# Hybrid decoder step on Trainium2: output-gate projections moved to the end and done in pairs by seven block products

## The chip, the cores and the metric

One core of a Trainium2 chip runs the whole program. The metric is the device time of one execution in microseconds, the median of several runs. The engines of the core work side by side, each through its own queue in order: TensorE (PE) multiplies matrices, VectorE (DVE) and ScalarE (ACT) do elementwise work, GpSimd (POOL) more of it, and SyncE (SP) issues the DMA transfers.

## The reference

One layer is applied to a prompt group (512 tokens) and a sample group (64 tokens); the kernel treats them as 576 tokens side by side.

```
proj = x @ w_in                       # 2048 -> 21904 columns
y_a = rwkv7(proj[..., :o1])           # RWKV-7 time mixing, 16 heads of 64
y_b = sliding_window_attention(...)   # y_c = mlstm(...), y_d = retention(...)
z    = silu(proj[..., o4:o5])         # 4 branches x 1024
gate = sigmoid(proj[..., o5:])        # 4 branches x 2048
for i, y_i in enumerate((y_a, y_b, y_c, y_d)):
    merged += gate[:, :, i] * ((y_i * z[:, :, i]) @ w_branch[i])
x_new = layer_norm(ALPHA * x + merged @ w_out)
```

In RWKV the state follows S <- S * w + sa (kk a)^T + v k^T token by token, with sa = -S kk. The kernel does this in chunks of 64 tokens, for which it needs the inverse of I + M1, M1 a strictly triangular 64 by 64 matrix for each head and chunk.

## The kernel before

**The projections.** w_in is cut into tiles of 128 columns; 171 of them are projections of x, among them 32 for z and 64 for the gates. x is kept on the chip transposed, as a high and a low part in float32r (xh, xl, 16 blocks of 128 rows). A projection (`dense_steps`, line 1285) loads its weights in two halves of 512 KB (raw, line 1297), splits each quarter in a high part on ScalarE (wh, line 1280) and a low part on VectorE (wl, line 1281), and multiplies: for each of 16 row blocks wh xh, wh xl and wl xh, each on two halves of the tokens of 288 columns, 96 matmuls in all, into one PSUM tile psd of two banks. One of the 16 row blocks, six matmuls, is a **step**.

**The stream.** Projections are one stream that TensorE works on between the mixers' own small products. `pump(n)` (line 1373) takes n steps. When a projection ends the next is taken from `asked`, the list that the mixers fill with projections of their own, or, if that is empty, from `work`: the 32 z and then the 64 gates, which wait for nothing. Each step of pump also advances `side`, a generator of other work, and what is left of finished projections. `need(name)` (line 1404) pumps until a projection is done. TensorE keeps the program's order, so a matmul that waits holds all that stand behind it, and pump is how other work is put in front of such a wait. The results of z and gates go to DRAM (zs, lines 1440 to 1456) and come back in phase 2. All DMAs here are issued by SP, in order: an issue that waits for its data holds the weight loads behind it.

**The RWKV mixer** (`branch_a`, line 198) takes two heads at a time, eight pairs j. `ask(j)` puts keys, receptances and values of the pair into `asked`. `prepare(j)` (line 282) makes normalised keys, decays and the array BK, with 32 steps of pump between its parts (FILL_SQUARES, FILL_SCAN, FILL_DECAY, FILL_NORM, FILL_BONUS) and needs for its own projections; the norms are taken to a power by GpSimd (nr). `grams(j)` (line 395) multiplies tokens against tokens, masks, sends M1 to DRAM (m1d) and reads it back to 126 partitions (MU, 3072 numbers each), 11 steps of pump in all. It then appends `invert` (line 367) to `side`: forward substitution on GpSimd, 63 rows, two instructions a row (lines tmp and TU), a row or so for each step of pump, then a store to DRAM (td, line 385) and loads into TT (line 390). `recur(j)` (line 486) first pumps until `side` is empty and then goes through eight chunks, each a chain of products with TT and the state and five steps of pump, and the sample group; 59 steps in all. Between prepare(j + 1) and recur(j) stand FILL_RECUR = 34 steps, and FILL_LAST = 110 ahead of the last recur.

**The other mixers** are sliding-window attention (line 589), mLSTM (841) and retention (1022). mLSTM and retention need a head's own projections at the head's start and ask for the next head's right behind that.

**The end.** What is left of `work` after retention runs while the first branch's inputs are loaded (`load_branch`, line 1484). Phase 2 multiplies the branches by w_branch (psd, line 1223), phase 3 is the output projection (pso) and the norm.

Of the kernel before, what the change touches and what calls it, by code (L numbers as in the profile page):

```python
# [19 lines left out]
P = 128  # L20
# [15 lines left out]
FIRST = {0: ("a_lo", 0), 1: ("a_k0", 0), 4: ("a_lo", 8)}  # L36
DECAY_C = 0.5 * float(np.exp(-0.5))

# [50 lines left out]
def _constants():  # L89
    """Tables that depend on shapes alone."""  # L90
# [18 lines left out]
    g, jj = i // 18, np.arange(10)  # L109
    c["tinit"] = (np.arange(64)[None, None] == (g[:, None] + 7 * jj[None])[:, :, None]).astype(f).reshape(P, 640)  # L110
# [37 lines left out]

CONST = _constants()
# [4 lines left out]
NG = 7  # L154
NJ = 10
# steps of the projections put between the steps of this branch
FILL_RECUR = 34
FILL_FIRST = 24
FILL_LAST = 110
# [38 lines left out]
def branch_a(S):  # L198
    with S.tc.tile_pool(name="bra", bufs=1) as pool:
        a = RwkvBranch(S, pool)  # L200
        a.prepare(0)
        S.pump(FILL_FIRST)
        a.grams(0)
        for j in range(8):
            if j < 7:
                a.ask(j + 1)
                a.prepare(j + 1)
                S.pump(FILL_RECUR)
            else:
                S.pump(FILL_LAST)  # L210
            a.recur(j)
            if j < 7:
                a.grams(j + 1)
        S.nc.sync.dma_start(out=S.O["o_shift"], in_=S.oshift)


class RwkvBranch:
    """Two heads at a time, in chunks of 64 tokens; the ninth chunk is the sample group.

    Rows of the arrays of a head pair: the even head's channels (or tokens) lie on partitions  # L220
    0..63 and the odd head's on 64..127; `ri` names the half that is not the head's own."""
# [6 lines left out]
    def __init__(self, S, pool):  # L228
# [7 lines left out]
        t = lambda name, shape: pool.tile([P] + shape, FP32, name=name)  # noqa: E731  # L236
# [3 lines left out]
        self.TT = t("TTbd", [9, 2, 64])  # L240
# [5 lines left out]
        for x in (self.TT, self.S0, self.U, self.Vb, self.Yn, self.bbd, self.kbd):  # L246
            S.G.memset(x, 0.0)
# [7 lines left out]
        self.ask(0)  # L255
# [8 lines left out]
    def ask(self, j):  # L264
        """the projections of a pair: keys, receptances and values (with 64 zeros on both sides)"""
        S = self.S

        def finish(n, col):
            def f(ps):
# [5 lines left out]
                x = self.tile("x" + n)  # L275
# [3 lines left out]
        for n, col in (("k", 8 + j), ("r", j), ("v", 16 + j)):  # L279
            S.ask(f"a_{n}{j}", finish(n, col), 256)  # L280

    def prepare(self, j):
# [4 lines left out]
        # normalised keys  # L287
# [14 lines left out]
        # decay and learning rate  # L302
# [10 lines left out]
        # running sums of the decays' logarithms  # L313
# [24 lines left out]
        r, vx = S.need(f"a_r{j}"), S.need(f"a_v{j}")  # L338
        v = vx[:, 64:64 + T]
# [5 lines left out]
        # bonus of the current token  # L345
# [4 lines left out]
        S.pump(FILL_BONUS)  # L350
        for a in range(0, T, SPL):
# [15 lines left out]
    def invert(self, st, mua, mub, tu, tmp):  # L367
        """forward substitution, one row of the unknowns' right side after another"""
        S, n = self.S, 18 * NG
        for _ in range(ROWS_BEFORE):  # L370
            yield 1
        for i in range(63):
            a = min(i // NG + 1, NJ)
            w = 63 - i
            row = mua[0:n, i, i + 1:64] if i < 32 else mub[0:n, i - 32, i - 31:32]
            S.tt(tmp[0:n, 0:a, 0:w], tu[0:n, 0:a, i:i + 1].to_broadcast([n, a, w]),
                 row.unsqueeze(1).to_broadcast([n, a, w]), eng=S.G)
            S.tt(tu[0:n, 0:a, i + 1:64], tu[0:n, 0:a, i + 1:64], tmp[0:n, 0:a, 0:w], ALU.subtract, eng=S.G)
            if i % ROWS_PACE == ROWS_PACE - 1:
                yield 1  # L380
# [3 lines left out]
        td = S.dpool.tile([18, NJ, NG, 64], FP32, tag="td", name="td", bufs=2)  # L384
# [3 lines left out]
        TT = self.TT  # L388
        for h in range(2):
            S.paced(S.nc.sync.dma_start(out=TT[self.HALF[h], :, h],  # L390
                                        in_=td[9 * h:9 * h + 9].rearrange("c a g t -> (a g) c t")[0:64]))
        for _ in range(ROWS_AFTER):
            yield 1

    def grams(self, j):
# [9 lines left out]
        m1 = self.tile("e3", (9, 64))  # L405
# [3 lines left out]
        for c0, n in ((0, 4), (4, 4), (8, 1)):  # L409
# [7 lines left out]
            for h in range(2):  # L417
# [4 lines left out]
                b1 = lambda x: x.unsqueeze(1).to_broadcast([64, n, 64])  # noqa: E731  # L422
                tt(m1[rs, c0:c0 + n], pv[rs, :, 0], b1(mk[rs, 0]))
# [7 lines left out]
        # inverse of I + M1, transposed: rows (group, head, chunk), each group every seventh row  # L431
        m1d = S.dpool.tile([18, 3072], FP32, tag="m1d", name="m1d", bufs=2)
        for h in range(2):
            d = m1d[9 * h:9 * h + 9]
            nc.sync.dma_start(out=d[:, 0:2048].rearrange("c (i t) -> i c t", i=32), in_=m1[64 * h:64 * h + 32])
            nc.sync.dma_start(out=d[:, 2048:].rearrange("c (i t) -> i c t", i=32),
                              in_=m1[64 * h + 32:64 * h + 64, :, 32:64])
        mu = self.tile("MU", (3072,))
        mua, mub = mu[:, 0:2048].rearrange("p (i t) -> p i t", i=32), mu[:, 2048:].rearrange("p (i t) -> p i t", i=32)
        tu = self.tile("TU", (NJ, 64))  # L440
        tmp = self.tile("tmp", (NJ, 64))
        nc.sync.dma_start(out=tu, in_=S.I["c_tinit"].rearrange("p (a b) -> p a b", a=NJ))
        nc.sync.dma_start(out=mu[0:18 * NG], in_=m1d.unsqueeze(0).broadcast_to([NG, 18, 3072]))
        S.side.append(self.invert(st, mua, mub, tu, tmp))
        # tokens on partitions
# [30 lines left out]
        # the sample group's queries, masked to each batch  # L476
# [9 lines left out]
    def recur(self, j):  # L486
        S, nc, st = self.S, self.S.nc, self.st.pop(j)
        V, G, act, tt, stt, mm, tr, pm = S.V, S.G, S.act, S.tt, S.stt, S.mm, S.tr, S.pm
        Z, BN, SV, TT, U, S0, dl = self.Z, self.BN, self.SV, self.TT, self.U, self.S0, st["dl"]
        while S.side:  # L490
            S.pump(1)
# [7 lines left out]
        two = lambda x: x.rearrange("p a b -> p (a b)")  # noqa: E731  # L499
# [29 lines left out]
        # the sample group  # L529
# [32 lines left out]
        # norm of each head (the even head's tokens on partitions 64..127)  # L562
# [26 lines left out]
def branch_b(S):  # L589
    nc, V, mm, tr, act, tt, stt, pm = S.nc, S.V, S.mm, S.tr, S.act, S.tt, S.stt, S.pm  # L590
    with S.tc.tile_pool(name="brb", bufs=1) as pool:
# [84 lines left out]
        def outputs(j, s):  # L676
            # probabilities with keys on partitions
# [29 lines left out]
        # the sample group: (KV head, query head, token) on partitions  # L707
# [46 lines left out]
def gate_rows(S, pool, dpool):  # L754
    """mLSTM gates, heads on partitions 0..7; returns the per-token rows the heads need"""
# [59 lines left out]
    # rows to every partition, by way of DRAM  # L815
# [4 lines left out]
    # tokens on partitions: [., 0:8] li - F, [., 32:40] weights of the state, [., 64:72] exp(-m)  # L820
# [20 lines left out]
def branch_c_heads(S, fmd, scd, cols):  # L841
    nc, V, mm, act, tt, stt, pm = S.nc, S.V, S.mm, S.act, S.tt, S.stt, S.pm
    with S.tc.tile_pool(name="brc", bufs=1, reuse_waits="tile") as pool:
# [4 lines left out]
        def conv(j, ps):  # L848
            """causal convolution of four taps and silu; twice its value"""
# [38 lines left out]
        for j in range(4):  # L888
            q2, k2 = S.need(f"c_q{j}"), S.need(f"c_k{j}")
            vcs = [S.need(f"c_v{2 * j + e}") for e in range(2)]  # L890
            if j < 3:
                ask(j + 1)
            # row factors on every partition
# [20 lines left out]
            # keys with tokens on partitions, weighted for the state  # L914
# [58 lines left out]
                # the sample group  # L973
# [27 lines left out]
def rope(S, pool, ps, cos, sin, half, name, bufs=2):  # L1001
    """x cos + (x with its halves swapped) sin, channels on partitions"""
# [19 lines left out]
def branch_d(S):  # L1022
    nc, V, mm, act, tt, stt, pm = S.nc, S.V, S.mm, S.act, S.tt, S.stt, S.pm
    with S.tc.tile_pool(name="brd", bufs=1) as pool:
# [18 lines left out]
        for h in range(8):  # L1043
            qr, kr, vc = S.need(f"d_q{h}"), S.need(f"d_k{h}"), S.need(f"d_v{h}")
            if h < 7:
                ask(h + 1)
            S.pump(6)
            # queries with their decay
# [5 lines left out]
            # keys and values with tokens on partitions  # L1054
# [14 lines left out]
            # scores, keys on partitions  # L1069
# [12 lines left out]
            # outputs, chunk after chunk, and the states  # L1082
# [19 lines left out]
            # the sample group: one state for each batch  # L1102
# [23 lines left out]
def head_out(S, pool, o, i, h, which, den=None):  # L1126
    """norm over the head's 128 values (tokens on partitions), transposed, gain and bias"""
# [33 lines left out]

@with_exitstack
def hybrid_kernel(ctx: ExitStack, tc: tile.TileContext, I, O):
# [3 lines left out]
    class InOrder:  # L1167
        """an engine whose instructions keep the order of the program"""
# [14 lines left out]
    class Behind:  # L1183
        """an engine whose instructions stay behind the last weight split before them"""
# [42 lines left out]
    def mm(out, lhsT, rhs, start=True, stop=True):  # L1227
# [495 lines left out]
```

## Time and profile before

| | us |
|---|---|
| median of 3 runs | 3391.16 |
| lowest to highest | 3389.91 to 3391.79 |
| span of the profiled execution | 3394.3 |

The profile is of one execution of its own; its span from the first to the last instruction is that execution's time, 3.1 us above the median of the runs. Stages as the trace has them, in us from the span's start: x comes in until about 32, RWKV until 1525, attention until 1814, mLSTM until 2231, retention until 2733, the rest of the stream until 2762, phase 2 until 3171, phase 3 to the end.

How to read the rows. In the table of windows a row has the stretch, its length, then for PE, PEld (weight load), DVE, ACT and POOL the busy us and the count of instructions, then the granted TensorE clock, the DMA engines' busy share and GB/s; with a filter on one tile and engine it has that engine alone. In the list of waits a row has who waited for whom, the total in us, how often and the longest. A group of instructions has line, engine, operation, output <- inputs, partitions x elements, count | busy us, mean ns of one | idle time before them and what ended it. In a timeline a row has start and duration in us and, in brackets, the idle time ahead of it. In the chain of work a row has start, length, engine and tile, and how many instructions were merged.

### The profile page before, as it was taken

What the parts mean: (1) busy time and instruction counts of PE and PEld (TensorE: products, weight loads), DVE (VectorE), ACT (ScalarE), POOL (GpSimd) and SP (SyncE); (2) the same over time, 40 slices, a digit from 0 to 9 for tenths busy, and PEclk for the clock granted to TensorE, in tenths of its full rate; (3) what the DMA queues carried; (4) which work ended last, traced back from release to release, by engine and by line L of the source; (5) the groups of instructions that cost most, each with busy time, mean ns of one, the idle gap of its engine ahead of it and who ended that gap; (6) DMA issues with size and microseconds to landing.
All of it is one profiled execution on the core that took longest, in us unless ns stands there. A gap on an engine that the chain in (4) does not pass through costs nothing.

```text
span 3394.3 us, 59113 instructions
## 1 busy us (share of the span) xinstructions
PE 3292.9 (97%) x24166; PEld 3160.5 (93%) x24166; DVE 1561.2 (46%) x3322; ACT 993.5 (29%) x2023; POOL 696.9 (21%) x1133
## 2 busy tenths in 40 slices
PE   8989998999899999999999999999999999999998
PEld 8979998989899899999999999999999999999886
DVE  5534454544444443334653455533343344555435
ACT  4323232323232323223443222222222222222211
POOL 0434435261708071611310000000000000000000
PEclk9989999999999999999999999999999999999999
DMA  5323232323231323334323333233333365554523
GB/s 166 110 82 108 95 115 84 113 89 111 87 106 63 115 91 107 112 101 133 93 90 107 94 96 95 88 123 119 101 102 115 97 197 184 184 171 132 171 79 106
DMA packets 174144, 384.67 MB, mean 113 GB/s; under 512 B 63704, under 2 KB 67544, under 8 KB 172272
## 3 DMA queue, kind: packets, MB, share of 16 engines
q1 hardware_dynamic: 173872, 380.88, 35.5%
q8 instruction: 190, 3.11, 0.4%
q14 instruction: 82, 0.67, 0.1%
HBM read 316.32 MB, written 58.11 MB: 110 GB/s over the span
## 4 chain that ended last, share of the span: by engine, by line
PE 73%; POOL 15%; DMA 6%; issue 3%; DVE 2%; SPq 1%; ACT 0%; POOLq 0%; ACTq 0%; DVEq 0%
PE psd L1177 45%; PE psd L1223 12%; PE pm L1177 10%; POOL TU L1177 7%; POOL tmp L1177 7%; PE pso L1223 6%; DMA MU<-m1d 3%; DMA raw<-in_wi 1%; DMA td<-TU 0%; POOL nr L1177 0%; DMA TTbd<-td 0%; DMA m1d<-e 0%; DMA raw<-in_wo 0%; DVE e L1193 0%; DVE wl L1281 0%
## 5 line engine op out<-in xcount | busy, mean ns | idle before, releaser
L1177 PE MATMUL psd<-xh,wh 128*128 128x288 f32 (+1 forms) x5472 | 1231.2, 306 | 10.1 <-ACT wh L1280 9.7
L1177 PE MATMUL psd<-xh,wl 128*128 128x288 f32 (+1 forms) x5472 | 1182.4, 297 | 31.7 <-DVE wl L1281 31.7
L1177 PE MATMUL psd<-xl,wh 128*128 128x288 f32 (+1 forms) x5472 | 1181.9, 297 | 0.0
L1281 DVE TENSOR_TENSOR wl<-raw,wh 128x512 fp32r<-128x512 f32 x812 | 595.7, 736 | 945.0 <-ACT wh L1280 928.9
L1280 ACT ACTIVATE wh<-raw 128x512 fp32r<-128x512 f32 x812 | 510.9, 631 | 1601.9 <-PE psd L1177 1218.0
L1177 PEld LDWEIGHTS psd<-xh,wl 128*128 128x128 f32 x5472 | 893.3, 190 | 33.7 <-DVE wl L1281 33.7
L1177 PEld LDWEIGHTS psd<-xh,wh 128*128 128x128 f32 x5472 | 883.4, 190 | 41.3 <-issue 14.5
L1177 PEld LDWEIGHTS psd<-xl,wh 128*128 128x128 f32 x5472 | 892.2, 190 | 0.0
L1177 POOL TENSOR_TENSOR tmp<-TU,MU 126x112 f32<-126x112 f32 (+49 forms) x504 | 262.7, 521 | 381.2 <-DMA MU<-m1d 342.9
L1177 POOL TENSOR_TENSOR TU<-TU,tmp 126x112 f32<-126x112 f32 (+49 forms) x504 | 263.5, 523 | 39.5
L1223 PE MATMUL psd<-yl,wh 128*128 128x288 f32 x1024 | 219.5, 295 | 0.0
L1223 PE MATMUL psd<-yh,wl 128*128 128x288 f32 x1024 | 219.4, 295 | 0.0
L1223 PE MATMUL psd<-yh,wh 128*128 128x288 f32 x1024 | 219.3, 295 | 0.0
L1177 POOL TENSOR_TENSOR rstd<-rstd,mhalf 128x5 f32<-128x5 f32 (+1 forms) x24 | 36.0, 1502 | 727.0 <-DVE rstd L1193 727.0
L1223 PEld LDWEIGHTS psd<-yh,wl 128*128 128x128 f32 x1024 | 164.6, 189 | 0.0
L1223 PEld LDWEIGHTS psd<-yh,wh 128*128 128x128 f32 x1024 | 164.6, 189 | 0.0
L1223 PEld LDWEIGHTS psd<-yl,wh 128*128 128x128 f32 x1024 | 164.6, 189 | 0.0
L1177 POOL TENSOR_TENSOR rs<-rs,mhalf 128x1 f32<-128x1 f32 (+1 forms) x5 | 4.5, 901 | 656.5 <-DVE rs L1193 656.5
L1177 POOL TENSOR_TENSOR smp<-Vbd,c_mrow 64x512 f32<-64x512 f32 x16 | 16.6, 1040 | 429.2 <-PE pm L1177 428.6
L1223 PE MATMUL pso<-w3h,mh 128*128 128x512 f32 x260 | 102.6, 395 | 1.4 <-ACT w3h L1193 1.4
L1223 PE MATMUL pso<-w3l,mh 128*128 128x512 f32 x260 | 103.3, 397 | 0.2 <-DVE w3l L1193 0.2
L1177 POOL TENSOR_TENSOR rsw<-rsw,c_sin 128x576 f32<-128x576 f32 x25 | 38.7, 1548 | 306.3 <-DMA rsw<-rx 306.3
(331 smaller groups left out, 2916.6 us busy)
## 6 DMA issues: line engine op xcount, KB each, us to landing
raw<-in_wi SPq DMA_DIRECT2D x342, 512.0 KB
raw<-in_wb SPq DMA_DIRECT2D x64, 512.0 KB
gd<-zs SPq DMA_DIRECT2D x64, 288.0 KB
th<-gd SPq DMA_DIRECT2D x64, 288.0 KB
raw<-in_wo SPq DMA_DIRECT2D x32, 512.0 KB
MU<-m1d SPq DMA_DIRECT2D x8, 1512.0 KB
zsd<-zs SPq DMA_DIRECT2D x32, 288.0 KB
ya<-yd SPq DMA_DIRECT2D x32, 288.0 KB
```

Of the source, the lines that this page charges most:

```text
L1177: ins = f(*a, **k).ins
L1223: PE.matmul(out=out, lhsT=lhsT, rhs=rhs, start=start, stop=stop)
L1280: a = nc.scalar.activation(out=wh, in_=src, func=ACTF.Copy)
L1281: b = nc.vector.tensor_tensor(out=wl, in0=src, in1=wh.bitcast(FP32), op=ALU.subtract)
```

## The change

RWKV: the FILL_RECUR and FILL_LAST steps go. Keys and receptances of pair j + 2 are asked for before recur(j), values of j + 1 at the start of grams(j). The part of the grams that gives M1 is computed a second time in a new `triangle`, right behind prepare, and the inversion starts from there, a recur and a grams ahead of its use (two TT buffers). The inversion is of two blocks of 32 (31 rows on 108 partitions, MU of 1024 numbers, 11 by 32 unknowns); the off-diagonal block is joined by nine transposes and two times 18 small products on TensorE. mLSTM and retention ask for the next head's projections before they need their own.

```diff
         a.prepare(0)
+        a.triangle(0)
+
+        a.ask(1, "kr")
         S.pump(FILL_FIRST)
         a.grams(0)
         for j in range(8):
             if j < 7:
-                a.ask(j + 1)
                 a.prepare(j + 1)
-                S.pump(FILL_RECUR)
-            else:
-                S.pump(FILL_LAST)
+
+                a.triangle(j + 1)
+            if j < 6:
+                a.ask(j + 2, "kr")
             a.recur(j)
...
-ROWS_BEFORE = 8
-ROWS_PACE = 5
-ROWS_STORE = 4
-ROWS_LOAD = 4
-ROWS_AFTER = 3
+ROWS_BEFORE = 18
+ROWS_STORE = 2
+ROWS_LOAD = 8
+ROWS_AFTER = 6
+ROWS_JOIN = 2
...
+        for c0, m in ((0, 4), (4, 4), (8, 1)):
+            ps = pm()
+            for c in range(m):
+                tr(ps[:, c * P:c * P + P], TT[:, c0 + c].rearrange("p a b -> p (a b)"), S.ident)
...
+                mm(ps[h][down[h], HB * c:HB * c + HB], m12[up[h], c], t11[up[h], c])
...
+                mm(ps[h][up[h], HB * c:HB * c + HB], g[down[h], c], TT[down[h], c, h, HB:64])
...
+    def triangle(self, j):
+
+        S, nc, st = self.S, self.S.nc, self.st[j]
+        V, act, tt, mm, pm = S.V, S.act, S.tt, S.mm, S.pm
+        while S.side:
+            S.pump(1)
+        m1 = self.tile("e3", (9, 64))
+        for c0, n in ((0, 8), (8, 1)):
+            S.pump(1)
+            ps = [pm() for _ in range(2)]
+            for c in range(n):
+                t0 = 64 * (c0 + c)
+                for h in range(2):
+                    rs = self.HALF[h]
+                    mm(ps[h][rs, 64 * c:64 * c + 64], st["bk"][rs, c0 + c, h], st["kk"][rs, t0:t0 + 64])
...
+        S.side.append(self.invert(self.TT[j % 2], mu, tu, tmp, m12))
...
-        while S.side:
+        while j == 7 and S.side:
             S.pump(1)
```

The stream's end: after retention two more projections run the old way (BEFORE_SEVEN = 2) while `input_forms` loads x again and makes four sums of its blocks, three of them as high and low parts at once. The rest of `work` goes to `Seven`. With two projections as rows of blocks A and the halves of x (rows and tokens) as blocks B, a pair is seven products of 8 row blocks, 288 tokens and three terms, fourteen units of 12 matmuls; four sums of weight blocks, 128 by 1024 numbers each in two instructions, are made by GpSimd, and results are summed by VectorE from two PSUM tiles and one more bank. Splits are made two units ahead. AFTER_SEVEN = 2, and one more where the number is odd, run singly while `load_branch(0)` loads.

```diff
+        b11, b12, b21, b22 = (x[:, i, j * SPL:j * SPL + SPL] for i in range(2) for j in range(2))
+        tm = pool.tile([P, 3, SPL], FP32, tag="tm", name="tm")
+        th, tl = (keep.tile([P, 3, SPL], F32R, name=f"{n}{k}") for n in ("fh", "fl"))
+        tt(t1[:, k], b12, b11, ALU.subtract, eng=G)
+        tt(tm[:, 1], b22, b12, ALU.subtract, eng=G)
+        tt(tm[:, 0], b22, t1[:, k], ALU.subtract)
+        tt(tm[:, 2], b21, tm[:, 0], ALU.subtract)
...
+        adds(u - 4, "S1", "A21", "A22", ALU.add, new=True)
+        adds(u - 2, "S2", "S1", "A11", ALU.subtract, new=True)
+        adds(u + 2, "A21", "A11", "A21", ALU.subtract)
+        adds(u + 4, "A12", "A12", "S2", ALU.subtract)
+
+        for src, b, which, first, last in (("A11", "B11", "X", 1, 0), ("A12", "B21", "Z", 1, 1),
+                                           ("S2", "T2", "X", 0, 0), ("S1", "T1", "W", 1, 0),
+                                           ("A21", "T3", "X", 0, 0), ("A12", "B22", "W", 0, 1),
+                                           ("A22", "T4", "X", 0, 1)):
...
+    rest = work[BEFORE_SEVEN:]
+    work[:] = work[:BEFORE_SEVEN]
+    with tc.tile_pool(name="conv", bufs=2, reuse_waits="tile") as vpool:
+        side.append(input_forms(S, vpool, tpool, seven, t1))
+        while side or work or len(current) > 1 or current[0][3] < 12:
+            pump(1)
+    spool = forms.enter_context(tc.tile_pool(name="blocks", bufs=1, reuse_waits="tile"))
+    stream = Seven(S, seven, t1, spool, evpool, rest)
+    stream.begin()
+    while current or finishing:
+        pump(1)
+    stream.pairs()
+    forms.close()
...
     ys = load_branch(0)
-    while current or work or finishing:
-        pump(1)
+    stream.tail()
```

More of the change, by code (lines that the diff above doesn't have):

```diff
@@ L146, in _constants @@
     return c
+HB = 32
+NG = 3
+NJ = 11
 CONST = _constants()
@@ L239, in __init__ @@
         self.SV = t("SV", [9, 2, 64])
-        self.TT = t("TTbd", [9, 2, 64])
+        self.TT = [t(f"TTbd{n}", [9, 2, 64]) for n in range(2)]
         self.S0 = t("S0bd", [8, P])
@@ L245, in __init__ @@
         self.bbd, self.kbd = t("bbd", [P]), t("kbd", [P])
-        for x in (self.TT, self.S0, self.U, self.Vb, self.Yn, self.bbd, self.kbd):
+        for x in (*self.TT, self.S0, self.U, self.Vb, self.Yn, self.bbd, self.kbd):
             S.G.memset(x, 0.0)
@@ L262, in tile, with ask @@
         return self.pool.tile([P] + list(shape), dt, tag=tag, name=tag, bufs=bufs)
-    def ask(self, j):
+    def ask(self, j, which):
         S = self.S
@@ L274, in f @@
                     return shift_mix(S, self.pool, ps, col, x[:, 64:64 + T], x)
-                x = self.tile("x" + n)
+                x = self.tile("x" + n, bufs=2 if n == "r" else 1)
                 return shift_mix(S, self.pool, ps, col, x, x)
             return f
-        for n, col in (("k", 8 + j), ("r", j), ("v", 16 + j)):
-            S.ask(f"a_{n}{j}", finish(n, col), 256)
+        for n in which:
+            S.ask(f"a_{n}{j}", finish(n, dict(k=8, r=0, v=16)[n] + j), 256)
     def prepare(self, j):
@@ L337, in prepare @@
             tt(kk[:, ts], kk[:, ts], ps[:, 0:ts.stop - ts.start])
-        r, vx = S.need(f"a_r{j}"), S.need(f"a_v{j}")
-        v = vx[:, 64:64 + T]
+        r = S.need(f"a_r{j}")
         t2 = sq
@@ L350, in prepare @@
         S.pump(FILL_BONUS)
+        vx = S.need(f"a_v{j}")
+        v = vx[:, 64:64 + T]
         for a in range(0, T, SPL):
@@ L387, in invert @@
             yield 1
-        TT = self.TT
         for h in range(2):
-            S.paced(S.nc.sync.dma_start(out=TT[self.HALF[h], :, h],
-                                        in_=td[9 * h:9 * h + 9].rearrange("c a g t -> (a g) c t")[0:64]))
+            for b in range(2):
+                r0, c0 = 64 * h + HB * b, 18 * h + 9 * b
+                S.paced(S.nc.sync.dma_start(out=TT[r0:r0 + HB, :, h, HB * b:HB * b + HB],
+                                            in_=td[c0:c0 + 9].rearrange("c a g t -> (a g) c t")[0:HB]))
@@ new lines, in invert @@
+        for _ in range(ROWS_JOIN):
+            yield 1
+        ps = [pm() for _ in range(2)]
+        for c in range(9):
+            for h in range(2):
+                mm(ps[h][down[h], HB * c:HB * c + HB], m12[up[h], c], t11[up[h], c])
+        two = lambda x: x.rearrange("p c t -> p (c t)")
+        act(two(g[down[0]]), ps[0][down[0], 0:9 * HB], scale=-1.0)
+        V.tensor_scalar(out=two(g[down[1]]), in0=ps[1][down[1], 0:9 * HB], scalar1=-1.0, scalar2=None, op0=ALU.mult)
+        for _ in range(ROWS_JOIN):
+            yield 1
@@ new lines, in invert @@
+        ps = [pm() for _ in range(2)]
+        for c in range(9):
+            for h in range(2):
+                mm(ps[h][up[h], HB * c:HB * c + HB], g[down[h], c], TT[down[h], c, h, HB:64])
+        for h in range(2):
+            pv = ps[h][up[h], 0:9 * HB].rearrange("p (c t) -> p c t", c=9)
+            if h == 0:
+                act(TT[up[h], :, h, HB:64], pv)
+            else:
+                V.tensor_copy(out=TT[up[h], :, h, HB:64], in_=pv)
+        for _ in range(ROWS_JOIN):
+            yield 1
@@ L403, in grams @@
             act(Z[rs, :, h, self.SLOT_R[h]], ch(st["r"]))
-        m1 = self.tile("e3", (9, 64))
+        if j < 7:
+            self.ask(j + 1, "v")
         xs = self.tile("XS", (2, 64))
@@ L430, in grams @@
                     tt(xs[ri], pv[ri, 0], mk[ri, 1:3])
[L432 to L444, printed above, removed]
         S.pump(FILL_TOKENS)
@@ L1159, in head_out, with input_forms, load @@
     S.finish_y(i, h, y)
+def input_forms(S, pool, keep, seven, t1):
+    V, G, act, tt = S.V, S.G, S.act, S.tt
+    xs = {}
+    def load(k):
+        xs[k] = pool.tile([P, 2, T], FP32, tag="xs2", name="xs2")
+        S.paced(S.nc.sync.dma_start(out=xs[k], in_=S.I["xT"][:, k::8]))
+    load(0)
+    yield 1
+    for k in range(8):
+        if k < 7:
+            load(k + 1)
+        yield 1
+        x = xs.pop(k)
+        b11, b12, b21, b22 = (x[:, i, j * SPL:j * SPL + SPL] for i in range(2) for j in range(2))
[5 more added lines that the diff above has]
+        tt(tm[:, 2], b21, tm[:, 0], ALU.subtract)
+        yield 1
+        act(th, tm)
+        tt(tl, tm, th.bitcast(FP32), ALU.subtract)
+        seven.th.append(th)
+        seven.tl.append(tl)
+        yield 1
@@ L1225, in hybrid_kernel, with mm @@
     ordered = InOrder(PE)
-    def mm(out, lhsT, rhs, start=True, stop=True):
-        ordered.matmul(out=out, lhsT=lhsT, rhs=rhs, start=start, stop=stop)
+    def mm(out, lhsT, rhs, start=True, stop=True, **k):
+        ordered.matmul(out=out, lhsT=lhsT, rhs=rhs, start=start, stop=stop, **k)
     def paced(ins):
@@ L1474, in hybrid_kernel @@
         branch(S)
+    evpool = p1.enter_context(tc.tile_pool(name="ev", bufs=1, side="right", reuse_waits="tile"))
+    forms = ExitStack()
+    tpool = forms.enter_context(tc.tile_pool(name="forms", bufs=1, side="right", reuse_waits="tile"))
+    t1pool = forms.enter_context(tc.tile_pool(name="t1", bufs=1, reuse_waits="tile"))
+    seven = SimpleNamespace(th=[], tl=[])
+    t1 = t1pool.tile([P, 8, SPL], FP32, name="t1")
+    rest = work[BEFORE_SEVEN:]
[11 more added lines that the diff above has]
+    forms.close()
     mpool = ctx.enter_context(tc.tile_pool(name="merged", bufs=1, reuse_waits="tile"))
```

217 lines of the change are left out of this document (195 added, 22 removed).

## The prediction

> **What bounds the kernel now.** I read the page first (span, busy times), then the table of windows by stage, then the waits of TensorE in the first mixer's stage.
>
> ```profile
> span 3394.3 us, 59113 instructions
> PE 3292.9 (97%) x24166; PEld 3160.5 (93%) x24166; DVE 1561.2 (46%) x3322; ACT 993.5 (29%) x2023; POOL 696.9 (21%) x1133
> 97.00:1525.00 1428.00, 1350.78 (x10146) 1306.79 (x10144) 647.22 (x1479) 422.70 (x907) 589.86 (x1055) 0.97 0.31 99
> 2231.00:2733.00 502.00, 502.00 (x3807) 493.60 (x3806) 184.22 (x397) 132.18 (x252) 32.81 (x24) 1.00 0.35 111
> 2733.00:2762.00 29.00, 29.00 (x220) 29.00 (x219) 14.81 (x21) 11.13 (x19) 0.00 (x0) 1.00 0.86 273
> PE psd L1177 <- DVE wl L1281: 31.7, 7, 7.8
> PE pm L1177 <- DMA TTbd<-td: 23.9, 3, 15.4
> PE pm L1177 <- DVE rsb L1193: 12.7, 3, 4.7
> PE pm L1177 <- DVE wl L1281: 4.5, 1, 4.5
> ```
>
> TensorE is the bound. Retention (2231 to 2733 us) has no idle time at all; RWKV (97 to 1525 us) has 1428.0 - 1350.8 = 77 us of it, nearly all in the four waits shown. So two things can make this kernel faster: fewer matmuls, or less of those 77 us. The terms below are of these two kinds, and of new waits.
>
> **How many projections reach the seven products.** A step of the stream is six matmuls, sixteen steps a projection. I counted the steps by following the calls of pump and need in program order, before and after. The activations that write a gate's tile check the count.
>
> ```profile
> 0.00:1525.00 1525.00, 43.58 (x68) 0.97 0.33 103
> 1525.00:1814.00 289.00, 4.46 (x7) 0.99 0.31 100
> 1814.00:2231.00 417.00, 5.74 (x9) 0.99 0.32 98
> 2231.00:2733.00 502.00, 5.71 (x9) 1.00 0.35 111
> ```
>
> My count for before gives 68, 7, 9 and 9 gate and output-gate projections in the four mixers: the same. For before, a head pair of RWKV takes 32 (prepare) + 11 (grams) + 59 (recur) + 34 (FILL_RECUR) + 40 (waits for its own keys and values) = 176 steps. For after, FILL_RECUR is gone, the waits are gone since keys and receptances were asked a pair earlier, and triangle adds 2: 104. In all RWKV ends at step 871 instead of 1467, retention at 1932 instead of 2684. 752 steps are 47 projections: 46 of the 96 are done by then, one is under way, 49 wait. Two go the old way, 47 remain: **22 pairs and 3 singles**.
>
> **The terms of the sum.** TensorE's prices first, from the chain of work in order of time.
>
> ```profile
> 2303.15 33.79 PE psd L1177 x252
> 613.33 2.01 PE pm L1177 x18
> 2719.43 4.23 PE pm L1177 x34
> ```
>
> (1) *Matmuls removed.* 33.79 / 252 = 0.134 us a matmul. A pair took 2 x 96 = 192; seven products of 8 row blocks by 3 terms are 168. 22 x 24 x 0.134 = **-70.8 us**. The three singles keep 96 each.
>
> (2) *Matmuls added in RWKV.* Triangle does 18 products of 64 by 64 by 64. The grams still compute the same block, so nothing is taken out in return. The nearest row is the grams' own, 2.01 us for 18 at twice the width: between 1.0 and 2.0 us. The join has 9 transposes and 36 products of 32 by 32. Retention's transposes and products are 4.23 / 34 = 0.124 us each: 1.1 us for the 9, and for the 36 at most 4.5, at least a quarter of that for blocks of a quarter the width. Together 3.2 to 7.6 us a pair; I take 4.5, a little below the middle, since the grams' products, which lie on the two halves of the array in turn, come out at 2.01 / 18 = 0.112, below 0.124. 8 x 4.5 = **+36 us** (26 to 61).
>
> (3) *Old waits that go.* What makes them:
>
> ```profile
> 517.58 0.69 DVE L1193 COPY e<-nr 128x512 f32<-128x512 f32 x1 [14.42 <-POOL nr L1177]
> DVE e L1193 <- POOL nr L1177: 78.0, 7, 14.4
> SPq L385 <- POOL TU L1177: 145.3, 8, 20.5
> L1177 POOL TENSOR_TENSOR tmp<-TU,MU 126x112 f32<-126x112 f32 (+49 forms) x504 | 262.7, 521 | 381.2 <-DMA MU<-m1d 342.9
> L1177 POOL TENSOR_TENSOR TU<-TU,tmp 126x112 f32<-126x112 f32 (+49 forms) x504 | 263.5, 523 | 39.5
> L1177 POOL TENSOR_TENSOR TU<-TU,tmp 126x62 f32<-126x62 f32 x8 | 2.4, 296 | 0.6
> 645.46 12.74 DMA MU<-m1d
> 200.99 4.96 DMA td<-TU
> 206.66 3.07 DMA TTbd<-td
> 696.74 0.75 PE L1177 MATMUL psd<-xh,wl 128*128 128x256 f32 x2 [2.71 <-DVE wl L1281]
> 697.29 0.68 PE L1177 MATMUL psd<-xh,wh 128*128 128x256 f32 x2
> ```
>
> The inversion takes (262.7 + 263.5) / 8 = 66 us of GpSimd a pair. The power for the key norms is queued behind its rows, VectorE stands 14.4 us on that, and the next weights' low part comes late: that is the 31.7. The store of TU stands in SP's queue for the last row, up to 20.5 us with weight loads behind it; then TT lands late: that is the 41. After, a pair has 31 rows of at most 96 and mostly some 62 elements, two instructions each, instead of 63 rows: 62 x 0.30 = 19 us, 24 with what lies between instructions. MU is 432 KB instead of 1512 KB, so its load takes perhaps 4 us of the 12.74. Load, rows, store and TT: 4 + 24 + 5 + 3 = 36 us; half as much again, for m1's way out and recur's own GpSimd work, makes 54. The cover from triangle to the first transpose is 65 steps of 6 x 0.134 = 0.80 us, 52 us, and recur's small products on top. The rows lie in recur, so the next pair's power finds GpSimd free. So both kinds of wait go: **-77 us**. After a gap TensorE also runs slow for a while: in the last two rows two matmuls take 697.29 - 696.74 = 0.55 us, against 0.27 (two of the 0.134 above). I take 2 us of such half speed, about 1.1 us lost, for each of the 14 gaps: **-15 us**.
>
> The Trainium skill, "TensorE: Matmul & The Clock Gate" (HAM oscillation — how this bites in real kernels), puts the limit at idle gaps of about 3.4 us. The trace disagrees: 2.71 us was enough. By the page the next term would be some 10 us smaller.
>
> (4) *New waits in RWKV.* What FILL_RECUR and the 40 waiting steps covered is late next. Triangle's products need BK, the last thing that VectorE makes in prepare, and stand one step behind the bonus:
>
> ```profile
> 484.00:545.00 61.00, 52.99 (x383) 51.60 (x382) 36.22 (x68) 17.08 (x32) 54.17 (x90) 0.94 0.19 64
> 536.14 0.67 PE L1177 MATMUL pm<-e,dmr 128*128 128x288 f32 x3 [0.20 <-DVE e L1193]
> 536.90 0.81 DVE L1193 TENSOR_TENSOR bo<-pm,xv 128x288 f32<-128x288 f32 x2
> 537.63 0.74 DVE L1193 SCALAR_TENSOR_TENSOR BK<-e,e 64x576 f32<-64x576 f32 x1
> ...
> 539.32 0.93 DVE L1193 SCALAR_TENSOR_TENSOR BK<-e,e 64x576 f32<-64x576 f32 x1
> 540.16 0.99 DVE L1193 TENSOR_TENSOR BK<-xk,e 64x576 f32<-64x576 f32 x1
> ```
>
> The first row is the window of this prepare: VectorE is busy 36.2 of 61 us and held 14.4 of the rest. The bonus ends at 536.8, one step ends at 537.5, BK's odd half is there at 540.2 to 541.2: TensorE waits 2.7 to 3.7 us, say 3.2. The eight steps for the values also stood between the norm and the bonus; without them VectorE's chain (six passes of 0.7 to 1.0 us and two weight splits) is some 2 us longer than the 6.4 us of FILL_BONUS. The join's evacuations have two steps of cover each and a busy VectorE before them: 1 us a pair, and recur's first solve 0.5. With 1.3 us of slow clock: 8 us a pair, **+64 us**. Bounds: 2 us a pair if VectorE, no longer held 14 us, runs ahead (+16); 20 if its whole prepare chain comes to lie on the path (+160).
>
> (5) *Into the stage of pairs.*
>
> ```profile
> 0.00:32.00 32.00, 24.43 (x157) 23.86 (x158) 17.41 (x25) 16.36 (x20) 4.23 (x12) 1.00 0.84 274
> raw<-in_wi SPq DMA_DIRECT2D x342, 512.0 KB
> xs<-in_xT SPq DMA_DIRECT2D x7, 576.0 KB
> L1281 DVE TENSOR_TENSOR wl<-raw,wh 128x512 fp32r<-128x512 f32 x812 | 595.7, 736 | 945.0 <-ACT wh L1280 928.9 <-PE pm L1177 13.2
> L1280 ACT ACTIVATE wh<-raw 128x512 fp32r<-128x512 f32 x812 | 510.9, 631 | 1601.9 <-PE psd L1177 1218.0 <-PE psd L1223 236.4 <-DMA raw<-in_wi 86.2
> L1177 POOL TENSOR_TENSOR res<-res,ln 128x512 f32<-128x512 f32 x2 | 3.1, 1554 | 1.2 <-ACT res L1193 1.1
> ```
>
> input_forms reads x again: 8 x 576 KB, 4.7 MB, and 2 MB for the first pair's weights follow in memory that the forms give free. At the 274 GB/s of the first window with the stream's own 1.5 MB that is 30 us, against 36 steps, 29 us; A11 is third in the queue and its split comes after: I take **+10 us** (0 to 25). Inside the stage a pair is 168 x 0.134 = 22.5 us of TensorE. GpSimd's eight sums are 8 x 1.55 = 12.4, VectorE's 14 splits 10.3, ScalarE's 8.8 with some 3 more each for copies and closing; weights and stores are 2.7 MB, 119 GB/s. All of it lies beside TensorE's 22.5 us; a split is made two units of 1.6 us ahead of its use and takes 0.63 + 0.74. Asking earlier in mLSTM and retention costs nothing: the head's own 64 and 48 steps fill the stream as before. The three singles (3 x 12.9 us) cover the first branch's loads, which had 29 us and no gap.
>
> **Sum.** -70.8 + 36 - 77 - 15 + 64 + 10 = -53: a span of 3341. The profiled execution is 3.1 us above the median of the runs (3391.2), so I predict **3338 us**.
>
> **Rivals.** *VectorE runs ahead* (0.20). For it: it is busy 647 of 1428 us. Against it: prepare's passes depend on one another. With the lower bound of (4): 3338 - 48 = 3290. *The removed steps were the cover* (0.16): prepare becomes VectorE's chain, 20 us a pair instead of 8: 3338 + 96 = **3434, slower than before**. It decides from 8 + 53 / 8 = 15 us of new waiting a pair. For it: in the 47 us of that prepare in which VectorE wasn't held it was busy 36. Against it: part of that was arrears from being held. *The seven products don't pay* (0.06): GpSimd's sums and VectorE's splits exclude one another and a pair is paced by 12.4 + 10.3 + 3 = 25.7 us, what two projections cost before: 3338 + 71 = 3409. Against it: in the window of prepare GpSimd was busy 54 of 61 us, and the same pass on BK took 0.74 and 0.93 us there, so passes stretch by a quarter rather than add. "SBUF — State Buffer" of the Trainium skill (Who interferes with whom) states that rival's rule: a VectorE instruction with two SBUF inputs and a GpSimd one that reads SBUF exclude one another for the whole instruction; no row here shows a whole block.
>
> **Chances.** Forecast, 3305 to 3370: 0.50; VectorE ahead, below 3305: 0.20; between forecast and no change: 0.08; cover gone: 0.16; not paid: 0.06. What this kernel's timing can tell from no change is about 0.2%, 7 us. Of the 0.08, 0.05 is faster and 0.03 the same; the last two are slower. Faster 0.75, same 0.03, slower 0.22. Range 3275 to 3410: the low end is the lower bounds of (2) and (4) with (5) at 0, the high end takes in the third rival but not the second.
>
> **What would show it.** (1): some 528 fewer stream matmuls, 0.134 apart, with TensorE without gaps over 22 pairs. (2): the small products' time in RWKV up by 36. (3): no wait on TTbd or behind nr. (4): a gap ahead of triangle's products that ends with BK. (5): one gap before the first pair that ends with a weight load. What would make it wrong: a transpose of TT that waits for its DMA in every pair, a count of pairs far from 22, or a pair much longer than 22.5 us.

## The result, and the profile after

The changed kernel takes **3447.5 us** (median of 4 runs, 3444.2 to 3455.4) against 3391.5 us for the kernel before on the same chip: ratio 1.0167, 95% interval 1.0148 to 1.0187. It is slower by 1.7%, where 3338 us was forecast; the time lies above the range too. The profiled spans differ by 3442.4 - 3394.3 = 48 us.

The page of the changed kernel, the span and the engines' busy times:

```profile
span 3442.4 us, 60678 instructions
...
PE 3285.5 (95%) x24574; PEld 3123.8 (91%) x24574; DVE 1813.9 (53%) x3587; ACT 1127.4 (33%) x2313; POOL 667.6 (19%) x814
```

TensorE is still the bound by its share, but that share has fallen from 97% to 95%: it is busy 7 us less and idle 55 us more. The count of its records rises by 24574 - 24166 = 408. The trace has 936 more small products in RWKV, and so 528 fewer matmuls of the stream, 22 pairs times 24, exactly as forecast. The products were saved; the time was lost in between. The table of windows says where (span, busy time and count of PE, PEld, DVE, ACT, POOL, then granted clock, DMA share, GB/s). The windows are RWKV, then the two projections after retention in which x is read again together with the first eight units of the pairs, and then the rest of the pairs with the first of the single projections. In the timeline the pairs' first product starts at 2155.7 us and their last ends at 2764.9:

```profile
97.00:1047.00 950.00, 911.74 (x7539) 862.04 (x7538) 531.54 (x1362) 328.13 (x775) 270.17 (x543) 0.98 0.27 83
2123.00:2197.00 74.00, 52.98 (x335) 50.40 (x334) 45.34 (x51) 23.23 (x41) 33.35 (x30) 0.85 0.48 148
2197.00:2778.00 581.00, 512.27 (x3676) 492.40 (x3675) 345.61 (x373) 240.97 (x436) 256.89 (x162) 1.00 0.32 103
```

- **The pairs** take 26.4 us each: 2544 matmuls are done in the 400 us from 2300 to 2700 (the row is shown under e1_own_banks), and a pair has 168. At 0.134 us a matmul they would be 22.5. That is 3.9 us a pair, 86 us in all. Two projections the old way took 25.7 us, so the pairs lose 0.7 us each instead of gaining 3.2. The clock is 1.00 here: these are plain gaps.
- **The transition** has 335 matmuls, 44.9 us at 0.134, and takes 74: 29 us of gaps and of slow clock (0.85).
- **RWKV** has 950.0 - 911.7 = 38 us of idle time in place of 77, and a mean clock of 0.98 in place of 0.97.

The waits of TensorE in the window of the pairs (what it waited for: us in total, times, longest):

```profile
PE psd L1470 <- ACT p L1486: 22.8, 23, 2.3
PE psd L1470 <- ACT u L1486: 19.7, 21, 0.9
PE psd L1470 <- ACT wh L1573: 14.1, 22, 0.6
PE psd L1470 <- DVE rb L1486: 12.1, 22, 0.6
```

Four gaps a pair, each once in every pair (the longest, 2.3 us, belongs to a single projection). Three of them end not with a weight but with an engine that *reads a sum*: p and u are ScalarE's copies of a finished part of a sum, rb is VectorE's addition. No product needs p, u or rb as an input. The timeline around two of them (start, duration, engine, line, operation, output and inputs; in brackets the idle time and what ended it):

```profile
2303.43 0.29 PE L1470 MATMUL psd<-xh,wl 128*128 128x288 f32 x1
...
2303.68 0.63 ACT L1573 ACTIVATE wh<-raw 128x512 fp32r<-128x512 f32 x1 [0.97 <-PE psd L1470]
2304.22 0.39 ACT L1486 ACTIVATE p<-psd 128x288 f32<-128x288 f32 x1
...
2304.66 0.40 PE L1470 MATMUL psd<-fh,wh 128*128 128x288 f32 x1 [0.94 <-ACT p L1486]
...
2307.83 0.29 PE L1470 MATMUL psd<-fh,wl 128*128 128x288 f32 x1
...
2308.16 0.46 DVE L1486 TENSOR_TENSOR rb<-psd,p 128x288 f32<-128x288 f32 x1 [0.33 <-PE psd L1470]
...
2308.68 0.40 PE L1470 MATMUL psd<-xh,wh 128*128 128x288 f32 x1 [0.55 <-DVE rb L1486]
```

At 2303.7 us the product of the weight sum S1 with the form T1 is complete in W. The next product, A21·T3, goes into X, another bank. Its first weights have been ready since 2301.9, yet it starts at 2304.66, when the copy of W is done, and that copy stood behind a weight split on ScalarE. Four microseconds later it is the other way round: A12·B22 goes into W and waits until VectorE has read X. The code says why:

```python
    def bank(self, s, which):
        if which not in s:
            if which == "Z":
                s["Z"] = S.pm()
            else:
                d = S.psd.tile([P, 2, 512], FP32, tag="d", name="psd")
                s["X"], s["W"] = d[:, 0], d[:, 1]
        ...
```

X and W are the two halves of **one** tile. Two gaps of a pair stand where the products change from X to W, two where they change back.

### The profile page after: what moved, and what is told of

It reads as the page before. It is cut to its first block, busy times and chain, and to the rows that moved or that the text cites. A ratio compares the mean times of both kernels' runs of the same rounds, so it can differ in the third digit from the quotient of the medians.

```text
span 3442.4 us, 60678 instructions
## 1 busy us (share of the span) xinstructions
PE 3285.5 (95%) x24574; PEld 3123.8 (91%) x24574; DVE 1813.9 (53%) x3587; ACT 1127.4 (33%) x2313; POOL 667.6 (19%) x814
## 5 line engine op out<-in xcount | busy, mean ns | idle before, releaser
L1470 PE MATMUL psd<-xh,wh 128*128 128x288 f32 (+1 forms) x4592 | 1101.0, 310 | 45.7 <-ACT u L1486 20.6
L1470 PE MATMUL psd<-xh,wl 128*128 128x288 f32 (+1 forms) x4592 | 1043.8, 297 | 10.5 <-DVE wl L1574 10.3
L1470 PE MATMUL psd<-xl,wh 128*128 128x288 f32 (+1 forms) x4592 | 1045.0, 298 | 0.0
L1470 PEld LDWEIGHTS psd<-xh,wh 128*128 128x128 f32 x4592 | 757.3, 191 | 87.6 <-ACT u L1486 25.7
L1470 PEld LDWEIGHTS psd<-xh,wl 128*128 128x128 f32 x4592 | 770.6, 190 | 12.1 <-DVE wl L1574 12.0
L1470 PEld LDWEIGHTS psd<-xl,wh 128*128 128x128 f32 x4592 | 770.5, 190 | 0.0
L1470 PE MATMUL psd<-fh,wh 128*128 128x288 f32 x528 | 160.3, 304 | 39.8 <-ACT p L1486 20.5
L1470 PE MATMUL psd<-fh,wl 128*128 128x288 f32 x528 | 157.7, 299 | 0.3 <-DVE wl L1574 0.3
L1470 PE MATMUL psd<-fl,wh 128*128 128x288 f32 x528 | 156.5, 296 | 0.0
L1470 PEld LDWEIGHTS psd<-fh,wh 128*128 128x128 f32 x528 | 100.6, 190 | 49.8 <-ACT p L1486 25.7
L1574 DVE TENSOR_TENSOR wl<-sn,wh 128x512 fp32r<-128x512 f32 x88 | 132.7, 1527 | 22.5 <-ACT wh L1573 20.4
```

The lines of the kernel that those rows point to most:

```text
L1470: ins = f(*a, **k).ins
L1574: b = nc.vector.tensor_tensor(out=wl, in0=src, in1=wh.bitcast(FP32), op=ALU.subtract)
```

## The experiments

Three theories. *Theory 1*: the program orders writes and reads of psd by the whole tile, so a product into one half waits for the reader of the other half; that is the 3.9 us a pair. *Theory 2*, the third rival of the prediction: GpSimd's sums and VectorE's splits exclude one another and pace a pair. *Theory 3*, its second rival: RWKV lost its cover. All ratios are to the kernel before on the same chip, with 95% intervals.

### X and W in tiles of their own (e1_own_banks)

```diff
-            if which == "Z":
-                s["Z"] = S.pm()
+            if which == "X":
+                s["X"] = S.psd.tile([P, 2, 512], FP32, tag="d", name="psd")[:, 0]
             else:
-                d = S.psd.tile([P, 2, 512], FP32, tag="d", name="psd")
-                s["X"], s["W"] = d[:, 0], d[:, 1]
+                s[which] = S.pm()
```

> Only change: of a pair's three sums X, W and Z, the two that were halves of one psd tile (X and W) become tiles of their own, so a product into W no longer waits for the read of X, nor one into X for the read of W. Theory 1 (the shared tile is what makes a pair 26.4 us instead of 22.5): the four gaps of a pair go, the waits on p, u and rb (22.8 + 19.7 + 12.1 us) all but vanish, a pair takes 22.5 to 23 us, the stage of pairs 581 us becomes about 500, the time about 3365 us. Theory 2 (GpSimd's sums and VectorE's splits exclude one another and pace a pair with 12.4 + 10.3 + 3 = 25.7 us): the gaps move to the weights (wh, wl), a pair stays at 26 us, the time within 10 us of 3447. Theory 3 (RWKV's removed cover): no change, 3447.

**3351.5 us, ratio 0.9873 (0.9858 to 0.9888).** From 1.7% slower to 1.3% faster, by an edit that changes no operation and no order. The window 2300 to 2700 us, all of it pairs, first in the changed kernel, then in this one:

```profile
2300.00:2700.00 400.00, 353.50 (x2544) 339.80 (x2544) 245.00 (x258) 166.94 (x303) 195.06 (x123) 1.00 0.32 102
```

```profile
2300.00:2700.00 400.00, 400.00 (x3015) 400.00 (x3015) 304.74 (x305) 195.33 (x355) 206.67 (x130) 1.00 0.40 125
```

46.5 us of gaps are now none, and in the same time 471 more matmuls are done: 400 / 3015 x 168 = 22.3 us a pair instead of 26.4. The span falls by 92 us: some 86 to 90 from the pairs (3.9 or 4.1 us each), and the single projections at the end, whose X and W shared a tile in the same way, had two gaps of 2.3 and 1.8 us. The fourth wait of the list above, put down to a weight split (wh), is gone as well: VectorE's read of W ended beside that split.

### The same sharing for another two sums (e4_x_and_z_share)

```diff
-            if which == "Z":
-                s["Z"] = S.pm()
+            if which == "W":
+                s["W"] = S.pm()
...
-                s["X"], s["W"] = d[:, 0], d[:, 1]
+                s["X"], s["Z"] = d[:, 0], d[:, 1]
```

> As the changed kernel, but X and Z are the halves of one psd tile and W is a tile of its own. Theory 1 (a product into one half waits for the read of the other half, through the shared tile) expects the gaps to move: one where Z begins, ending with the copy p1 of X (about 0.9 us), one where X goes on after Z, ending with VectorE's read of Z (about 0.6 us), and none between X and W; a pair of 24 to 25 us instead of 26.4, the time about 3400 us. If it were the reading of PSUM itself, by any engine at any time, that holds the products up, the four gaps stay and the time is 3447.

**3402.6 us, ratio 1.0038 (1.0026 to 1.0051)**, and the waits of TensorE in the window of its pairs:

```profile
PE psd L1470 <- DVE ra L1486: 21.9, 21, 1.1
PE psd L1470 <- ACT p L1486: 19.7, 21, 0.9
```

Two gaps a pair now, at the places where X and Z change; those between X and W are gone. From 2300 to 2700 us this kernel does 2708 matmuls, 24.8 us a pair, as theory 1 forecast. Physically all three sums lie in banks of their own in each of the three kernels, so it isn't the reading of PSUM that stops TensorE, but which sums the program holds as one object. The Trainium skill, "PSUM — Partial Sum Buffer" (Summary: rules for kernel authors), asks for a different bank, with semaphores by bank, where PSUM is read while a matmul runs. The banks were different here; the guard, by the tile of two banks, was coarser than that rule, and it cost 3.9 us a pair.

### The sums on GpSimd left out (e3_no_sums)

```diff
                     if new and g == 0:
-                        s[out] = self.spool.tile([P, 8, P], FP32, tag="sn", name="sn", bufs=3)
-                    G.tensor_tensor(out=s[out][:, gs], in0=s[a][:, gs], in1=s[b][:, gs], op=op)
+                        s[out] = s[a]
```

> GpSimd's sums of weight blocks left out (the products take unsummed blocks, so the gates are not the reference's); the same products, splits, copies and the shared psd tile stay. Theory 1 (shared tile): a pair stays at 25.5 us or more; only the transition gets shorter, by the waits on the sums, some 10 to 15 us: about 3432 us. Theory 2 (sums and splits exclude one another): a pair falls to 22.5 to 23 us, wl of the summed blocks from 1.5 to 0.74 us, the time to about 3360.

**3427.7 us, ratio 1.0092 (1.0074 to 1.0109)**: theory 1's number. The window of pairs of this kernel:

```profile
2300.00:2700.00 400.00, 355.57 (x2564) 341.99 (x2563) 168.71 (x259) 168.14 (x305) 0.00 (x0) 1.00 0.33 105
```

GpSimd does nothing, VectorE 76 us less, and a pair still takes 400 / 2564 x 168 = 26.2 us. So theory 2 doesn't pace the pairs. Its mechanism is real all the same. VectorE's groups in that window, of e1_own_banks and of this kernel (busy us, mean ns of one):

```profile
L1573 DVE TENSOR_TENSOR wl<-sn,wh 128x512 fp32r<-128x512 f32 x68 | 103.0, 1534 | 11.0 <-ACT wh L1572 9.4
```

```profile
L1573 DVE TENSOR_TENSOR wl<-sraw,wh 128x512 fp32r<-128x512 f32 x122 | 84.4, 692 | 114.5 <-ACT wh L1572 112.2
```

Beside sums a split takes 1.53 us, without them 0.69. VectorE has that time to spare: it is busy 305 of 400 us in e1_own_banks, which has no gap.

### The seven products left out (e2_no_seven)

```diff
-    rest = work[BEFORE_SEVEN:]
...
-    while current or finishing:
+    while len(work) > 2:
         pump(1)
-    stream.pairs()
...
-    stream.tail()
+    while current or work or finishing:
+        pump(1)
```

> The seven products left out: all gate projections go the old way one after another, everything else of the changed kernel (earlier asking, triangle, inverse by halves, join) stays. Theory 1 and 2 (the loss is in the stage of pairs): the time is that of the kernel before, within 10 us of 3391 (RWKV's saved waits and its added products cancel: -2 us counted by stage). Theory 3 (the removed steps were the cover, so RWKV pays): 3430 us or more.

**3394.5 us, ratio 1.0003 (0.9993 to 1.0012).** All that the change does to RWKV and the other mixers comes to 0 within 4 us. Theory 3 falls.

### The transition (e5_third_ahead, e6_form_in_halves)

In the changed kernel the waits of TensorE from 2123 to 2197 us begin with these:

```profile
PE psd L1470 <- DVE wl L1574: 10.6, 5, 8.7
PE psd L1470 <- ACT wh L1573: 5.2, 1, 5.2
```

5.2 us ahead of the first product with S2, whose blocks landed late, and 8.7 us ahead of the last of T1's products (in e1_own_banks 5.4 and 10.2). At the second, VectorE makes the low part of T1 (xl) out of two operands in SBUF. From 2172 to 2197 us in the changed kernel, beside GpSimd's sums, then in e3_no_sums, which has none:

```profile
L1486 DVE TENSOR_TENSOR xl<-t,xh 128x288 fp32r<-128x288 f32 x8 | 11.3, 1475 | 0.0
...
L1486 DVE TENSOR_TENSOR ra<-pm,p 128x288 f32<-128x288 f32 x1 | 0.4, 445 | 0.0
```

```profile
L1485 DVE TENSOR_TENSOR xl<-t,xh 128x288 fp32r<-128x288 f32 x8 | 3.0, 449 | 0.0
...
L1485 DVE TENSOR_TENSOR ra<-pm,p 128x288 f32<-128x288 f32 x1 | 0.5, 457 | 0.3 <-PE pm L1469 0.3
```

Eight passes take 11.3 us instead of 3.0, while a pass of the same size with one operand in PSUM (ra) keeps its 0.45 us. This is what the Trainium skill, "SBUF — State Buffer" (Who interferes with whom), states: an exclusive lock, and only between GpSimd and the VectorE instructions that use the shared port. In e3_no_sums, without the sums, the 8.7 us gap isn't there: from 2170 us on no wait of that kernel is above 0.9 us.

```diff
-BEFORE_SEVEN = 2
+BEFORE_SEVEN = 3
```

> X and W in tiles of their own as in e1_own_banks, and three projections instead of two go the old way before the pairs (22 pairs still, two single ones at the end instead of three). The same number of products, 12.9 us more cover for the second reading of x and the first weights. Theory A (what is left of the transition, 5.4 + 10.2 us of gaps, is loads and sums that come too late): the gap before the first product with S2 goes and the one before T1's products shrinks, 3351 - 5 to 15 = 3336 to 3346 us. Theory B (it is VectorE's passes on the T1 form that GpSimd's sums hold up wherever they meet): the second gap stays at about 10 us, 3346 us at best. If two single ones are too few for the first branch's loads, gaps of some us come up at the end.

**3338.9 us, ratio 0.9848 (0.9826 to 0.9871).** The gap ahead of S2 is gone (0.7 us left), the one before T1's products is 11.1 us: theory A for the first, theory B for the second.

```diff
-        self.at(self.before, 4, self.first_form)
+        for g in range(2):
+            self.at(self.before, 2 + 2 * g, lambda g=g: self.first_form(g))
...
-    def first_form(self):
+    def first_form(self, g):
...
-        for k in range(8):
+        for k in range(4 * g, 4 * g + 4):
```

> As e5_third_ahead, and the T1 form is made in two halves of four blocks, two units before each is needed, instead of all eight ahead of unit 4. Theory A: no further gain (0 to 2 us). Theory B: the second gap, still there in e5_third_ahead, shrinks by half or more, another 3 to 6 us, about 3337 us.

**3337.8 us, ratio 0.9847 (0.9824 to 0.9870).** The one gap becomes two, of 3.7 and 4.2 us. That is 3 us less of gaps, less than the half that theory B forecast, and the time can't be told from e5_third_ahead's.

### More cover ahead of triangle (e7_cover_for_bk)

```diff
-            S.pump(1)
+            S.pump(4 if n > 1 else 1)
             ps = [pm() for _ in range(2)]
```

> As e6_form_in_halves, and triangle takes four steps of the stream instead of one ahead of its first products. If the wait on BK is one of VectorE's delay (0.72 + 1.05 us a pair in the trace) it goes: 7 x 1.8 = 12 us, against 3 us since 21 instead of 22 pairs are left for the seven products: about 9 us less than e6_form_in_halves. If VectorE is the bound there (the removed steps were cover, theory 3) the steps only shift the wait to the next point: the same time, or up to 3 us more.

**3304.4 us, ratio 0.9744 (0.9725 to 0.9762).** 33 us less than e6_form_in_halves, where 9 were expected. The wait on BK was the largest of RWKV from 260 to 1000 us in e6_form_in_halves:

```profile
PE pm L1470 <- DVE BK L1486: 10.6, 12, 1.1
PE pm L1470 <- ACT Z L1486: 10.2, 6, 2.0
```

and none is left in this kernel, where the same list begins with

```profile
PE pm L1470 <- ACT Z L1486: 7.9, 6, 2.2
PE pm L1470 <- DVE SV L1486: 2.3, 6, 1.5
```

The windows of e6_form_in_halves, two short ones around a wait on Z of 1.6 us and the long one:

```profile
608.00:612.00 4.00, 2.51 (x31) 2.21 (x29) 2.59 (x6) 1.89 (x5) 0.00 (x0) 1.00 0.06 11
612.00:616.00 4.00, 3.91 (x19) 3.91 (x20) 1.12 (x6) 0.70 (x3) 0.00 (x0) 0.59 0.36 123
...
260.00:1000.00 740.00, 711.03 (x5860) 672.10 (x5859) 417.89 (x1057) 255.59 (x603) 201.62 (x409) 0.97 0.27 83
```

and the long one of e7_cover_for_bk:

```profile
260.00:1000.00 740.00, 725.04 (x6095) 687.56 (x6094) 425.60 (x1081) 262.73 (x621) 200.62 (x407) 1.00 0.28 87
```

The first two rows show what the expectation left out: that wait is followed by 4 us at a mean clock of 0.59, with 19 matmuls where 4 us at full speed hold 30 (4 / 0.134). Summed over these 740 us in windows of 4 us, the slow clock costs 18.8 us in e6_form_in_halves and 1.7 us here: eleven slow stretches of 1.7 us lost each become one. They don't follow every gap. Behind the two gaps on BK (0.72 and 1.05 us, one soon after the other) the slow clock came in five of six head pairs, behind single gaps of 1.5 to 2.0 us five times in nine, and behind the longest gap of this kernel, 2.2 us, it stayed at 1.00. Over the whole execution idle time falls by 17 us (75 to 58) and the slow clock, counted while TensorE is busy, by 19 (32 to 13). With 3 us back for the pair that no longer fits, that is the 33 measured.

### T1's low part on GpSimd, and its control (e8_form_on_gpsimd, e9_form_sooner)

The edit is shown against e7_cover_for_bk.

```diff
-            self.at(self.before, 2 + 2 * g, lambda g=g: self.first_form(g))
+            self.at(self.before, 2 * g, lambda g=g: self.first_form(g))
...
-            S.tt(lo, self.t1[:, k], h.bitcast(FP32), ALU.subtract)
+            S.tt(lo, self.t1[:, k], h.bitcast(FP32), ALU.subtract, eng=S.G)
```

> As e7_cover_for_bk, and the low parts of the T1 form are subtracted on GpSimd, in order with its sums, halves queued ahead of units 0 and 2. Theory B (VectorE's passes on that form and GpSimd's sums hold each other up): the two gaps of the transition (4.5 and 3.3 us) and the slow clock behind them (10 us at half speed) shrink to a few us, 6 to 12 us less: about 3295 us. Theory A (loads and sums are simply late): GpSimd gets eight more passes ahead of the sums that the first pair waits for, so the gaps stay or grow, 3304 us or up to 3312.

The control has the first of these two edits alone.

> As e7_cover_for_bk, and the two halves of the T1 form, still on VectorE, are queued ahead of units 0 and 2 instead of 2 and 4: the control for e8_form_on_gpsimd, with the same places in the queues. If the place is what counts, it gains what e8_form_on_gpsimd gains. If it is the two engines (theory B), 3304 us within 4.

**e8: 3296.2 us, ratio 0.9721 (0.9704 to 0.9738). e9: 3306.1 us, ratio 0.9736 (0.9712 to 0.9760).** The waits of TensorE from 2140 to 2200 us, first of e8_form_on_gpsimd, then of e9_form_sooner:

```profile
PE psd L1470 <- DVE wl L1574: 2.5, 4, 0.9
PE pm L1470 <- POOL xl L1470: 1.9, 2, 1.3
```

```profile
PE psd L1470 <- DVE wl L1574: 7.9, 3, 5.6
```

With the eight passes in GpSimd's own order the longest gap is 1.3 us; with the same places in the queue but on VectorE it is 5.6, now ahead of a product with S2. From 2120 to 2200 us e8_form_on_gpsimd does 541 matmuls at a clock of 1.00, e9_form_sooner 496 at 0.94. So the place didn't make the gap: passes on VectorE did. Taking them off VectorE also frees the 3.0 us that they take there with nothing beside them; but in e3_no_sums they stay on VectorE, without sums, and the gap isn't there. It takes both, passes on VectorE and sums on GpSimd. The medians differ by 10 us in the direction of theory B, but the intervals overlap: the trace decides here, the times alone wouldn't. e8_form_on_gpsimd is the fastest version of this study, 2.8% below the kernel before and 4.4% below the changed one (3296.2 / 3447.5).

## Why the prediction was wrong

**(1) Matmuls removed, -71: right.** 22 pairs, 3 single projections, 528 matmuls fewer, 0.134 us apart.

**(2) to (4), RWKV, +36 - 77 - 15 + 64 = +8: right in the sum**, 0 within 4 us by e2_no_seven. The terms, with the slow clock summed in windows of 4 us and counted only while TensorE is busy, since it costs nothing while TensorE waits anyway:
- The waits on TTbd and behind nr are gone but for single ones, as forecast.
- The slow clock was mis-sized. In the kernel before it costs 29 us in RWKV, not 15: a slow stretch costs 1.7 us, behind some gaps twice that, where 1.1 was taken.
- The new waits: 38 us idle and 18 of slow clock, 56 us for the 64 forecast. The wait on BK is 0.72 and 1.05 us a pair, not 3.2. The copies to Z on ScalarE, which the forecast didn't have, wait as much:

```profile
L1470 PE MATMUL pm<-e,BK 64*64 64x64 f32 x252 | 14.0, 247 | 10.6 <-DVE BK L1486 10.6
L1470 PE MATMUL pm<-c_ident,TTbd 128*128 128x128 f32 x72 | 13.3, 297 | 15.7 <-ACT Z L1486 11.9 <-DMA TTbd<-td 3.5 <-PE pm L1470 0.2
...
L1470 PE MATMUL pm<-t,m 32*32 32x32 f32 x288 | 7.8, 193 | 0.6 <-DVE t L1486 0.6
...
L1470 PE MATMUL pm<-TTbd,g 32*32 32x32 f32 x288 | 6.1, 192 | 0.0
```

- The small products: 14.0 + 13.3 + 7.8 + 6.1 = 41 us busy in this window, which has seven of the eight triangles; the eighth adds 2, so 43 for the 36 forecast. They take back what the waits gave: over the whole executions of the kernel before and of e2_no_seven idle time falls from 101 to 68 us and the slow clock from 33 to 27, 40 us together.

**(5) Into the stage of pairs, +10: this step failed.** Two of its statements:
- "All of it lies beside TensorE's 22.5 us." It did for the splits, the sums and the loads, as e1_own_banks shows. It didn't for the copies and additions that read the sums. The step counted their time on ScalarE ("some 3 more each for copies and closing") and never asked which product waits for a reader. Here each read of X or of W held up the products that went on into the other, because the two are one tile: 3.9 us x 22 = +86.
- The 10 us (0 to 25) for the transition were 29. The late loads were foreseen and cost 5.2 us. T1's low part, eight passes of VectorE beside GpSimd's sums, was not, nor the slow clock behind both gaps.

By the terms as measured, -71 + 0 + 86 + 29 = +44; the spans differ by 48, and the two gaps of the single projections make up 4.

**The rivals.** *VectorE runs ahead*: not in all. The wait on BK stayed in six of seven pairs; at 1.8 us it was near this rival's 2, but other waits, on the copies to Z above all, brought RWKV to 56 us where the rival had 16. *The removed steps were the cover*: no, by e2_no_seven. *The seven products don't pay* named the result, a pair that costs what two projections did, and its 25.7 us is near the 26.4 measured; but that is coincidence, for its mechanism was not the cause: without any sums a pair still took 26.2. The argument against it, that passes stretch by a quarter, was wrong too: beside sums they took 2.2 times as long, and there was time for it. The lock cost some 9 us at one place of the transition instead. The sentence on what would make the forecast wrong, "a pair much longer than 22.5 us", was the right alarm, and it had a cause that wasn't among the rivals.

**The range** ended at 3410: no case in it held a wait inside the pairs other than for the engines' time.

## What to carry to other kernels

When sums that are filled in turn are evacuated piece by piece, look at what the program takes as one object: two halves of a tile that are written and read in alternation wait for one another, though no data passes between them and no engine is short of time. For each product of a new order ask not only "are its inputs there" but also "who still reads what it is allocated with". And price a gap of 1.5 to 2 us on TensorE above its length: in the traces shown here about half of such gaps, and most of the close pairs of shorter ones, were followed by a slow clock that cost another 1.7 us, so that a few steps of filler ahead of it can be worth more than the gap.

## What the runs showed of the hardware

- The slow clock can follow gaps far below the about 3.4 us that the Trainium skill, "TensorE: Matmul & The Clock Gate" (HAM oscillation — how this bites in real kernels), gives as the limit: here 1.6 us was enough (clock 0.59 over the next 4 us). In 740 us of RWKV, e6_form_in_halves with 29 us idle and no wait above 2.0 us lost 18.8 us to it, e7_cover_for_bk with 15 us idle 1.7 us. It is no fixed rule of length: 2.2 us of idle time in e7_cover_for_bk had no slow clock behind it, and what decides is not shown.
- The lock between GpSimd and VectorE stretched passes to 2.2 times (1.53 for 0.69 us) and 3.3 times (1475 for 449 ns) their length, and left a pass with an operand in PSUM alone. It cost nothing over 22 pairs in which VectorE was 76% busy, and 8.7 to 11.1 us of idle TensorE at one place, where it waited for eight such passes in a row.
